# Scores of two chunks on four array quarters, level sums and low weight parts on GpSimd

## The chip, the cores and the metric

The kernel runs on one core of a Trainium2 chip. The metric is device time of one execution in microseconds: 2511.98 us, the median of three runs (2508.98 to 2515.89). One execution was recorded by the hardware profiler; it took 2509.05 us, of which 2507.3 us lie between its first and its last instruction (the span).

The engines have short names in the profile: PE is TensorE's matrix multiplication, PEld its weight loads, DVE is VectorE, ACT is ScalarE, POOL is GpSimd, and SP is SyncE, which here only issues DMAs.

## What is computed

Two transformer blocks work on one sequence of 1024 tokens of width 1024, all in fp32. The change lies in the second block, in its two gated linear attentions (four heads with 64 keys and 128 values, four heads with 64 keys and 64 values). With a cumulated log gate `b_cum` per token and key, every chunk of 64 tokens needs

```
scores = jnp.einsum('bhtd,bhsd,bhtsd->bhts', q_c, k_c, decay)   # decay = exp(b_t - b_s) for s <= t
o_c    = scores @ v_c + (q_c * exp(b_cum)) @ state
state  = exp(b_last) * state + (k_c * exp(b_last - b_cum)).T @ v_c
```

The decay depends on the pair of tokens and on the key, so the score is not one matrix product. The kernel halves the chunk six times: at level l, pairs whose tokens lie in the left and in the right half of the same piece of 64 >> l tokens are one product of k * exp(ref - b) and q * exp(b - ref), with ref the gate at the end of the left half. The diagonal is a seventh product, k with q.

Next to it the block has a projection (`w_in_2`, `w_values`), a stick-breaking attention, and an output projection (`w_out_2`).

## The kernel before

A large product in fp32 is three products in a faster format: a weight tile of 128x512 (`wr`, 256 KB) is split into a high part `wh` (ACT, L77) and a low part `wl` = wr - wh (DVE, L80), and PE multiplies hi with wl, lo with wh and hi with wh (L153, L773 to L775). `load_parts` does this for every tile, with three buffers for each of `wr`, `wh` and `wl`.

The second block is a set of Python generators, each of which yields a cost; `weave` always steps the one that is behind, and so writes one program out of four streams: `filler` (the projection's units, then the output rows), two streams `gated` (two pairs of heads each, per half of the sequence: `gla_a`, `gla_b`, `gla_c`), and `sticks`. A scheduler then orders each engine's instructions; on the chip every engine works its own list in order and waits on semaphores.

In `gla_b`, `gla_levels` makes the left and right operands of all six levels for four chunks (`XL`, 128x256 a level): two subtractions and two multiplications of 128x128 on DVE and one exponential of 128x256 on ACT for each level. Partitions 0 to 63 hold one head, 64 to 127 the other. Then, chunk by chunk, PE multiplies: levels 2 to 5 and the diagonal as 64x64 products (L1416, L1418), levels 1 and 0 as products of 16 and 32 columns (L1421), the two heads on two quarters of the array: rows 0 to 63 into PSUM partitions 0 to 63, and rows 64 to 127 into 64 to 127. Each chunk takes one of two PSUM buffers `s`, shared by both gated streams. DVE multiplies the five 64-column pieces with their masks (`mk`, 128x320, one buffer in each stream) and adds them up with a reduction (L1424) into `PT`, the stationary operand of the product with the values (L1445).

The trace records each fp32 product of this size as two MATMULs and two LDWEIGHTS: a product is two passes through its quarter.

Of the kernel before, what the change touches and what calls it, by code (L numbers as in the profile page):

```python
# [65 lines left out]
def tile_hybrid_blocks(ctx: ExitStack, tc: tile.TileContext, a: dict, out: bass.AP):  # L66
# [66 lines left out]

    def load_parts(src, shape):

        wr = wp.tile(shape, F32, tag="wr", name="wr")
        SY.dma_start(out=wr, in_=src)
        wh = wp.tile(shape, F32R, tag="wh", name="wh")
        wl = wp.tile(shape, F32R, tag="wl", name="wl")
        split(wh, wl, wr)  # L140
        return wh, wl
# [1146 lines left out]
    def gla_levels(half, jj, q, k, b, c0, c1):  # L1288
# [4 lines left out]
        q, k, b = q[:, n0:n0 + m], k[:, n0:n0 + m], b[:, n0:n0 + m]  # L1293
        for l in range(6):
# [7 lines left out]
            bl, br = v4(b)[:, :, 0, :], v4(b)[:, :, 1, :]  # L1302
            ref = bl[:, :, h - 1:h].to_broadcast([128, n, h])
            tt(v4(ar)[:, :, 0, :], ref, bl, SUB)
            tt(v4(ar)[:, :, 1, :], br, ref, SUB)
            act(ar, ar, AF.Exp, scale=1.0 / 16 if jj < 2 else 1.0)
            xl = v4(XL[:, l, :])
            tt(xl[:, :, 0, :], v4(k)[:, :, 0, :], v4(ar)[:, :, 0, :], MUL)
            tt(xl[:, :, 1, :], v4(q)[:, :, 1, :], v4(ar)[:, :, 1, :], MUL)
        return XL  # L1310

    def gla_a(half, jj):
# [13 lines left out]
        SY.dma_start(out=qk, in_=qk_d[half][jj].rearrange("a p t -> p a t"))  # L1326
        q, k = qk[:, 0, :], qk[:, 1, :]
# [54 lines left out]
    def gla_b(half, jj):  # L1382
# [18 lines left out]
        o = 0  # L1401
        for c in range(8):
            if c % 4 == 0:
                XL = gla_levels(half, jj, q, k, b, c, c + 4)
                yield YL * 4
                o = c
            cs = slice(c * 64, (c + 1) * 64)
            ps = pss_t([128, 5, 64])

            def xl(hb, l, c0, n):  # L1410
                return XL[hb:hb + 64, l, (c - o) * 64 + c0:(c - o) * 64 + c0 + n]


            for l in (2, 3, 4, 5):
                for hb in (0, 64):
                    T.matmul(out=ps[hb:hb + 64, l - 2, :], lhsT=xl(hb, l, 0, 64), rhs=xl(hb, l, 0, 64), start=True, stop=True)  # L1416
            for hb in (0, 64):
                T.matmul(out=ps[hb:hb + 64, 4, :], lhsT=k[hb:hb + 64, cs], rhs=q[hb:hb + 64, cs], start=True, stop=True)  # L1418
            for l, lc, rc, n in ((1, 0, 16, 16), (1, 32, 48, 16), (0, 0, 32, 32)):
                for hb in (0, 64):  # L1420
                    T.matmul(out=ps[hb + lc:hb + lc + n, 0, rc:rc + n], lhsT=xl(hb, l, lc, n), rhs=xl(hb, l, rc, n), start=True, stop=True)  # L1421
            mk = slot("mk", [128, 5, 64])
            tt(mk, ps, lvm, MUL)
# [308 lines left out]
```

## Time and profile before

| | |
|---|---|
| median of three runs | 2511.98 us (2508.98 to 2515.89) |
| the profiled execution | 2509.05 us, span 2507.3 us |
| busy share of the span | PE 95%, PEld 74%, DVE 67%, ACT 47%, POOL 4% |
| weave of the four streams | from about 1870 us to 2455 us of the span |
| mean granted TensorE clock | 0.981 of full speed |

An engine's busy time counts overlapping instructions once. A matmul's recorded length contains the time in which the array fills and drains, so the rate of a dense row of matmuls is read from the distance of their starts, not from their length.

### The profile page before, as it was taken

What the parts mean: (1) busy time and instruction counts of PE and PEld (TensorE: products, weight loads), DVE (VectorE), ACT (ScalarE), POOL (GpSimd) and SP (SyncE); (2) the same over time, 40 slices, a digit from 0 to 9 for tenths busy, and PEclk for the clock granted to TensorE, in tenths of its full rate; (3) what the DMA queues carried; (4) which work ended last, traced back from release to release, by engine and by line L of the source; (5) the groups of instructions that cost most, each with busy time, mean ns of one, the idle gap of its engine ahead of it and who ended that gap; (6) DMA issues with size and microseconds to landing.
All of it is one profiled execution on the core that took longest, in us unless ns stands there. A gap on an engine that the chain in (4) does not pass through costs nothing.

```text
span 2507.3 us, 40921 instructions
## 1 busy us (share of the span) xinstructions
PE 2375.0 (95%) x15310; PEld 1863.7 (74%) x15310; DVE 1688.9 (67%) x3678; ACT 1171.0 (47%) x2223; POOL 100.2 (4%) x138
## 2 busy tenths in 40 slices
PE   6989998889999999999999999999999999999997
PEld 5767776767777777778778887788877667777665
DVE  5466556667686776663885555555568988788887
ACT  4345433654433434343543333343345575656863
POOL 1001000100000000000000000000000000000000
PEclk9999999979999999999999999999999999999989
DMA  6433323555352342333463332243256335342446
GB/s 203 147 116 89 99 87 94 160 162 159 97 172 79 107 140 91 92 124 96 161 205 94 97 93 93 81 156 100 94 166 223 99 112 179 105 132 91 144 136 244
DMA packets 219997, 320.77 MB, mean 128 GB/s; under 512 B 56956, under 2 KB 95508, under 8 KB 219799
## 3 DMA queue, kind: packets, MB, share of 16 engines
q1 hardware_dynamic: 219798, 318.17, 40.5%
q8 instruction: 120, 1.97, 0.3%
q14 instruction: 79, 0.64, 0.1%
HBM read 270.88 MB, written 47.21 MB: 127 GB/s over the span
## 4 chain that ended last, share of the span: by engine, by line
PE 60%; DVE 9%; DMA 3%; issue 3%; ACT 2%; POOL 1%; SPq 0%; POOLq 0%; ACTq 0%; DVEq 0%
PE g L153 32%; PE d L153 12%; DVE wl L80 1%; PE s L1416 1%; PE R L1520 1%; PE gr L773 1%; DVE cv L83 1%; PE gr L774 1%; PE gr L775 1%; PE x L773 1%; PE x L775 1%; PE x L774 1%; DVE tmp L80 1%; PE z L1505 1%; PE po L1538 1%
## 5 line engine op out<-in xcount | busy, mean ns | idle before, releaser
L77 ACT ACTIVATE wh<-wr 128x512 fp32r<-128x512 f32 x712 | 442.8, 626 | 639.8 <-PE g L153 216.9
L153 PE MATMUL g<-hi,wl 128*128 128x512 f32 (+1 forms) x1680 | 677.1, 403 | 13.5 <-DVE lo L80 4.1
L153 PE MATMUL g<-hi,wh 128*128 128x512 f32 (+1 forms) x1680 | 667.2, 397 | 0.0
L153 PE MATMUL g<-lo,wh 128*128 128x512 f32 (+1 forms) x1680 | 665.5, 396 | 0.0
L80 DVE TENSOR_TENSOR wl<-wr,wh 128x512 fp32r<-128x512 f32 x712 | 484.7, 685 | 207.2 <-ACT wh L77 205.9
L153 PEld LDWEIGHTS g<-hi,wl 128*128 128x128 f32 (+1 forms) x1680 | 317.1, 189 | 91.0 <-issue 8.6
L153 PEld LDWEIGHTS g<-hi,wh 128*128 128x128 f32 (+1 forms) x1680 | 316.7, 188 | 71.7 <-issue 2.6
L153 PEld LDWEIGHTS g<-lo,wh 128*128 128x128 f32 (+1 forms) x1680 | 317.2, 189 | 68.5 <-issue 3.7
L83 DVE SCALAR_TENSOR_TENSOR cv<-g,CW,cv 128x511 f32<-128x511 f32 (+1 forms) x256 | 190.8, 745 | 179.3 <-ACT cv L77 179.0
L153 PE MATMUL d<-hh,wl 128*128 128x512 f32 x512 | 202.5, 399 | 12.7 <-ACT hh L77 7.5
L153 PE MATMUL d<-hl,wh 128*128 128x512 f32 x512 | 202.1, 395 | 0.1
L153 PE MATMUL d<-hh,wh 128*128 128x512 f32 x512 | 200.8, 392 | 0.0
L77 ACT ACTIVATE cv<-g,CW 128x512 f32<-128x512 f32 x128 | 99.5, 777 | 181.5 <-PE g L153 181.1
L80 DVE TENSOR_TENSOR acc<-d,acc 128x512 f32<-128x512 f32 x112 | 76.4, 689 | 94.7 <-PE d L153 94.6
L153 PEld LDWEIGHTS d<-hh,wl 128*128 128x128 f32 x512 | 95.8, 189 | 41.8 <-ACT hh L77 12.0
L153 PEld LDWEIGHTS d<-hl,wh 128*128 128x128 f32 x512 | 96.5, 188 | 23.0 <-DVE hl L80 3.6
L153 PEld LDWEIGHTS d<-hh,wh 128*128 128x128 f32 x512 | 96.6, 189 | 20.3 <-issue 0.2
L773 PE MATMUL gr<-wl,hi 128*128 128x512 f32 x200 | 83.4, 418 | 7.3 <-DVE wl L80 6.6
L774 PE MATMUL gr<-wh,lo 128*128 128x512 f32 x200 | 80.1, 400 | 0.0
L775 PE MATMUL gr<-wh,hi 128*128 128x512 f32 x200 | 79.7, 399 | 0.0
L127 POOL TENSOR_TENSOR rs<-ms,half_c 128x1 f32<-128x1 f32 x48 | 29.4, 612 | 1085.1 <-DVE ms L87 1077.2
L77 ACT ACTIVATE hh<-cv 128x512 fp32r<-128x512 f32 x64 | 40.4, 631 | 65.5 <-DVE cv L80 65.4
(508 smaller groups left out, 3475.7 us busy)
## 6 DMA issues: line engine op xcount, KB each, us to landing
wr<-in_w_up_dram SPq DMA_DIRECT2D x256, 256.0 KB, 2.7
wr<-in_w_in_dram SPq DMA_DIRECT2D x160, 256.0 KB, 2.9
wr<-in_w_down_dram SPq DMA_DIRECT2D x128, 256.0 KB, 2.6
wr<-in_w_out_dram SPq DMA_DIRECT2D x100, 256.0 KB, 3.0
wr<-in_w_values_dram SPq DMA_DIRECT2D x64, 256.0 KB, 2.9
wa<-in_w_ada_dram SPq DMA_DIRECT2D x24, 512.0 KB, 4.3
xt<-x SPq DMA_DIRECT2D x24, 512.0 KB, 4.5
xt<-in_x_dram SPq DMA_DIRECT2D x16, 512.0 KB, 3.6
```

What stands on the lines that cost most here:

```text
L77: S.activation(out=out, in_=in_, func=func, **kw)
L80: (eng or V).tensor_tensor(out=out, in0=in0, in1=in1, op=op)
L83: V.scalar_tensor_tensor(out=out, in0=in0, scalar=scalar, in1=in1, op0=op0, op1=op1)
L127: G.tensor_tensor(out=dst, in0=src, in1=half_c[0:src.shape[0], 0:src.shape[1]], op=ALU.pow)
L153: T.matmul(out=ps, lhsT=l, rhs=r, start=(first and n == 0), stop=(last and n == 3 * len(wk) - 1))
L773: T.matmul(out=p, lhsT=hi[:, k, tok], rhs=wl, start=first, stop=False)
L774: T.matmul(out=p, lhsT=lo[:, k, tok], rhs=wh, start=False, stop=False)
L775: T.matmul(out=p, lhsT=hi[:, k, tok], rhs=wh, start=False, stop=last)
L1416: T.matmul(out=ps[hb:hb + 64, l - 2, :], lhsT=xl(hb, l, 0, 64), rhs=xl(hb, l, 0, 64), start=True, stop=True)
L1505: T.matmul(out=z[:, h, :], lhsT=Ks[:, p, h, kb * 128:(kb + 1) * 128], rhs=q[:, h, off:], start=q is ql, stop=q is qh)
L1520: T.matmul(out=R[:, :, c0:c1], lhsT=m, rhs=x[:, :, c0 - off:c1 - off], start=start and x is sl, stop=x is sh, skip_group_check=not start)
L1538: T.matmul(out=po[hb:hb + 64, c0:c1], lhsT=Vh[:, kb, hd * 64:(hd + 1) * 64], rhs=ar[:, h, c0 - off:c1 - off], start=(kb == top), stop=(kb ...
```

## The change

Four things change, all in the second block.

The scores of two chunks are now multiplied together. The second chunk's heads go to the other two quarters: rows 0 to 63 into PSUM partitions 64 to 127, rows 64 to 127 into 0 to 63, in the second PSUM buffer. A pair of chunks takes both `s` buffers at once; the two heads of the second chunk lie swapped in PSUM and are swapped back when `PT` is written.

The sum over the levels is no longer a DVE reduction: POOL adds 128x128, then 128x64, and for the first chunk of a pair writes `PT` with a third addition; for the second chunk, two DVE additions of 64x64 write `PT`.

`gla_levels` makes one subtraction of 128x256 (b - ref on both halves), two exponentials of 128x128 with opposite scale, and one multiplication of 128x256 for each level. For the latter k and q lie side by side in one tile, in the order k, q, which two DMAs load instead of one.

In the weave of the four streams, `load_parts` makes the low part `wl` on POOL instead of DVE.

```diff
--- before.py
+++ after.py
@@ -131,13 +131,17 @@
         act(hi, src, AF.Copy)
         tt(lo, src, hi.bitcast(F32), SUB)
 
+
+    low_eng = [V]
+
     def load_parts(src, shape):
 
         wr = wp.tile(shape, F32, tag="wr", name="wr")
         SY.dma_start(out=wr, in_=src)
         wh = wp.tile(shape, F32R, tag="wh", name="wh")
         wl = wp.tile(shape, F32R, tag="wl", name="wl")
-        split(wh, wl, wr)
+        act(wh, wr, AF.Copy)
+        tt(wl, wr, wh.bitcast(F32), SUB, low_eng[0])
         return wh, wl
 
     def load_w(src, m=128):
@@ -1290,7 +1294,7 @@
         slot = rooms[jj < 2][0]
         n0, m = c0 * 64, (c1 - c0) * 64
         XL = slot("XL", [128, 6, m])
-        q, k, b = q[:, n0:n0 + m], k[:, n0:n0 + m], b[:, n0:n0 + m]
+        k, b = k[:, n0:n0 + m], b[:, n0:n0 + m]
         for l in range(6):
             h = 32 >> l
             n = m // (2 * h)
@@ -1299,14 +1303,14 @@
                 return t.rearrange("p (n s h) -> p n s h", s=2, h=h)
 
             ar = slot("tmp", [128, HALF], "ar")[:, 0:m]
-            bl, br = v4(b)[:, :, 0, :], v4(b)[:, :, 1, :]
-            ref = bl[:, :, h - 1:h].to_broadcast([128, n, h])
-            tt(v4(ar)[:, :, 0, :], ref, bl, SUB)
-            tt(v4(ar)[:, :, 1, :], br, ref, SUB)
-            act(ar, ar, AF.Exp, scale=1.0 / 16 if jj < 2 else 1.0)
-            xl = v4(XL[:, l, :])
-            tt(xl[:, :, 0, :], v4(k)[:, :, 0, :], v4(ar)[:, :, 0, :], MUL)
-            tt(xl[:, :, 1, :], v4(q)[:, :, 1, :], v4(ar)[:, :, 1, :], MUL)
+            ref = v4(b)[:, :, 0, h - 1:h].to_broadcast([128, n, 2 * h])
+            tt(ar.rearrange("p (n t) -> p n t", n=n), b.rearrange("p (n t) -> p n t", n=n), ref, SUB)
+            tau = 1.0 / 16 if jj < 2 else 1.0
+            for s in range(2):
+                act(v4(ar)[:, :, s, :], v4(ar)[:, :, s, :], AF.Exp, scale=tau if s else -tau)
+
+            kq = bass.AP(k.tensor, k.offset, [k.ap[0], [2 * h, n], [HALF + h, 2], [1, h]])
+            tt(v4(XL[:, l, :]), kq, v4(ar), MUL)
         return XL
 
     def gla_a(half, jj):
@@ -1323,8 +1327,9 @@
             return t.rearrange("p (c t) -> p c t", c=8)
 
         qk = slot("qk", [128, 2, HALF])
-        SY.dma_start(out=qk, in_=qk_d[half][jj].rearrange("a p t -> p a t"))
-        q, k = qk[:, 0, :], qk[:, 1, :]
+        for x in range(2):
+            SY.dma_start(out=qk[:, 1 - x, :], in_=qk_d[half][jj][x])
+        k, q = qk[:, 0, :], qk[:, 1, :]
 
         mn, e, b = tmp("mn"), tmp("e"), tmp("b")
         if is_g:
@@ -1398,31 +1403,42 @@
                                  start=True, stop=True)
                 yield YT
             stt(Sa[:, c + 1, 0:dv] if c < 7 else Sg[jj], Sa[:, c, 0:dv], ebl[:, c, :], kv[:, c % nb, :], MUL, ADD)
-        o = 0
-        for c in range(8):
+        for c in range(0, 8, 2):
             if c % 4 == 0:
                 XL = gla_levels(half, jj, q, k, b, c, c + 4)
                 yield YL * 4
-                o = c
-            cs = slice(c * 64, (c + 1) * 64)
-            ps = pss_t([128, 5, 64])
-
-            def xl(hb, l, c0, n):
-                return XL[hb:hb + 64, l, (c - o) * 64 + c0:(c - o) * 64 + c0 + n]
+
+            ps = [pss_t([128, 5, 64]) for _ in range(2)]
+            four = [(x, hb, hb ^ 64 * x) for x in range(2) for hb in (0, 64)]
+
+            def prod(l, at, lc, rc, n):
+                for x, hb, ob in four:
+                    if l < 6:
+                        o = (c % 4 + x) * 64
+                        kl, ql = XL[hb:hb + 64, l, o + lc:o + lc + n], XL[hb:hb + 64, l, o + rc:o + rc + n]
+                    else:
+                        o = (c + x) * 64
+                        kl, ql = k[hb:hb + 64, o:o + 64], q[hb:hb + 64, o:o + 64]
+                    T.matmul(out=ps[x][ob + lc:ob + lc + n, at, rc:rc + n], lhsT=kl, rhs=ql, start=True, stop=True)
 
 
             for l in (2, 3, 4, 5):
-                for hb in (0, 64):
-                    T.matmul(out=ps[hb:hb + 64, l - 2, :], lhsT=xl(hb, l, 0, 64), rhs=xl(hb, l, 0, 64), start=True, stop=True)
-            for hb in (0, 64):
-                T.matmul(out=ps[hb:hb + 64, 4, :], lhsT=k[hb:hb + 64, cs], rhs=q[hb:hb + 64, cs], start=True, stop=True)
+                prod(l, l - 2, 0, 0, 64)
+            prod(6, 4, 0, 0, 64)
             for l, lc, rc, n in ((1, 0, 16, 16), (1, 32, 48, 16), (0, 0, 32, 32)):
-                for hb in (0, 64):
-                    T.matmul(out=ps[hb + lc:hb + lc + n, 0, rc:rc + n], lhsT=xl(hb, l, lc, n), rhs=xl(hb, l, rc, n), start=True, stop=True)
-            mk = slot("mk", [128, 5, 64])
-            tt(mk, ps, lvm, MUL)
-            V.tensor_reduce(out=PT[:, c, :].unsqueeze(2), in_=mk.rearrange("p l t -> p t l"), axis=X, op=ADD)
-            yield YB
+                prod(l, 0, lc, rc, n)
+            for x in range(2):
+                mk = slot("mk", [128, 5, 64])
+                tt(mk, ps[x], lvm, MUL)
+
+                tt(mk[:, 0:2], mk[:, 0:2], mk[:, 2:4], ADD, G)
+                tt(mk[:, 0], mk[:, 0], mk[:, 1], ADD, G)
+                if x == 0:
+                    tt(PT[:, c], mk[:, 0], mk[:, 4], ADD, G)
+                else:
+                    for i0, o0 in ((0, 64), (64, 0)):
+                        tt(PT[o0:o0 + 64, c + 1], mk[i0:i0 + 64, 0], mk[i0:i0 + 64, 4], ADD)
+            yield YB * 2
         gls[half, jj] = (qt, V2, PT, Sa)
 
     def gla_c(half, jj):
@@ -1587,7 +1603,9 @@
         for half in range(2):
             yield from stick(half)
 
+    low_eng[0] = G
     weave(filler, Stream(gated(0), RG, AG), Stream(gated(2), RH, AG), Stream(sticks(), RS, AS))
+    low_eng[0] = V
     p3.close()
 
     p4 = ExitStack()
```

The lists of the engines, with what each instruction waits for. PE, between output rows and scores, before (one chunk: eight 64x64 products of the levels, two of the diagonal, six narrow ones):

```order
L773 MATMUL gr<-wl,hi 128x512
L774 MATMUL gr<-wh,lo 128x512
L775 MATMUL gr<-wh,hi 128x512
L1416 MATMUL s<-XL 64x64 x8
L1418 MATMUL s<-qk 64x64 x2
L1421 MATMUL s<-XL 16x16 x4
L1421 MATMUL s<-XL 32x32 x2
L773 MATMUL gr<-wl,hi 128x512 [waits DVE_49]
L774 MATMUL gr<-wh,lo 128x512 [waits Activation_49]
```

PE after, a pair of chunks between the projection and the stick-breaking sums (L1422 holds all score products now):

```order
L157 MATMUL g<-hi,wh 128x512
L1422 MATMUL s<-XL 64x64 [waits DVE_49]
L1422 MATMUL s<-XL 64x64
L1422 MATMUL s<-XL 64x64 [waits DVE_49,PE_49]
L1422 MATMUL s<-XL 64x64 x13
L1422 MATMUL s<-qk 64x64 x4
L1422 MATMUL s<-XL 16x16 x8
L1422 MATMUL s<-XL 32x32 x4
L1536 MATMUL R<-sl,rest_r 128x512
L1536 MATMUL R<-sh,rest_r 128x512
```

Twice the products now stand in one uninterrupted row, so PE goes over from wide to narrow products and back once for two chunks.

DVE, around the masks of two chunks, before (`mk` is the masked product, `ev` and `wl` belong to the filler):

```order
L80 TENSOR_TENSOR mk<-s,C_16659 128x320 [waits DVE_49,PE_49]
L1424 TENSOR_REDUCE PT<-mk 128x64 [waits DVE_49]
L80 TENSOR_TENSOR mk<-s,C_16659 128x320 [waits DVE_49,PE_49]
L80 TENSOR_TENSOR ev<-ev,g 128x512 [waits Activation_49]
L1424 TENSOR_REDUCE PT<-mk 128x64 [waits DVE_49]
L87 TENSOR_SCALAR tmp<-qk 128x512 [waits DMAHW3_49]
L80 TENSOR_TENSOR wl<-wr,wh 128x512 [waits DMAHW7_49,Activation_49]
```

DVE after, at one of the six pairs in which nothing stands between the masks:

```order
L83 SCALAR_TENSOR_TENSOR gt<-t,P,gt 128x256
L80 TENSOR_TENSOR mk<-s,C_16659 128x320 [waits PE_49]
L80 TENSOR_TENSOR mk<-s,C_16659 128x320 [waits DVE_49,PE_49,Pool_49]
L80 TENSOR_TENSOR PT<-mk 64x64 [waits DVE_49,Pool_49]
L80 TENSOR_TENSOR PT<-mk 64x64
L1394 COPY Sa<-Sg_16668 128x128 [waits PE_49]
L1468 TENSOR_REDUCE ssn<-tmp 128x4 [waits Activation_49]
```

The second mask and the last additions now wait for POOL, and whatever stands behind them on DVE waits with them.

POOL after, in the same place (before, its list there held only the small powers of L127):

```order
L80 TENSOR_TENSOR wl<-wr,wh 128x512 [waits DMAHW2_49,PE_49,Activation_49]
L80 TENSOR_TENSOR mk<-mk 128x128 [waits DVE_49]
L80 TENSOR_TENSOR mk<-mk 128x64 [waits Pool_49]
L80 TENSOR_TENSOR PT<-mk 128x64 [waits Pool_49]
L80 TENSOR_TENSOR mk<-mk 128x128 [waits DVE_49]
L80 TENSOR_TENSOR mk<-mk 128x64 [waits Pool_49]
L127 TENSOR_TENSOR rsn<-ssn,half_c 128x4 [waits DVE_49]
L80 TENSOR_TENSOR wl<-wr,wh 128x512 [waits DMAHW4_49,Activation_49]
```

Low parts and level sums stand in one list: a low part behind a sum waits for DVE's mask, and a sum behind a low part waits for its weights.

## Rows read from the trace of the kernel before

**Rows 1.** The page's part 4, the chain that ended last, by engine

```profile
PE 60%; DVE 9%; DMA 3%; issue 3%; ACT 2%; POOL 1%; SPq 0%; POOLq 0%; ACTq 0%; DVEq 0%
```

**Rows 2.** Busy time by stretch: stretch, length, PE, PEld, DVE, ACT, POOL (instructions), clock, DMA

```profile
1870.00:2455.00 585.00, 554.32 (x5129) 414.17 (x5128) 485.60 (x1133) 374.04 (x727) 21.32 (x20) 0.99 0.44 140
1884.00:2335.00 451.00, 436.45 (x4174) 329.78 (x4172) 375.38 (x906) 280.91 (x554) 14.48 (x14) 1.00 0.42 133
2335.00:2455.00 120.00, 105.93 (x883) 75.72 (x884) 98.77 (x201) 85.63 (x161) 6.84 (x7) 0.94 0.46 149
```

**Rows 3.** The same view, L1416's matmuls and weight loads alone

```profile
1884.00:2335.00 451.00, 44.46 (x896) 34.03 (x896) 1.00 0.42 133
```

**Rows 4.** PE's timeline around one chunk: start, length to the last end, line, count

```profile
2307.11 0.39 PE L153 MATMUL g<-lo,wh 128*128 128x512 f32 x1
2307.33 0.39 PE L153 MATMUL g<-hi,wh 128*128 128x512 f32 x1
2307.65 0.68 PE L1416 MATMUL s<-XL 64*64 64x64 f32 x16
2308.16 0.28 PE L1418 MATMUL s<-qk 64*64 64x64 f32 x4
2308.38 0.29 PE L1421 MATMUL s<-XL 64*16 64x16 f32 x12
2308.60 0.50 PE L1520 MATMUL R<-sl,rest_r 128*128 128x512 f32 x1
2308.94 0.40 PE L1520 MATMUL R<-sh,rest_r 128*128 128x512 f32 x1
```

**Rows 5.** PE's timeline in the first block, 64x64 products on other quarters

```profile
202.66 1.15 PE L576 MATMUL rb__1594<-TT,UV 64*64 64x64 f32 x32
...
205.96 0.68 PE L617 MATMUL ou<-St,AR 64*64 64x64 f32 x16
...
219.32 0.68 PE L626 MATMUL ou<-St,AR 64*64 64x64 f32 x8
```

**Rows 6.** Groups on DVE and ACT, 1870 to 2455 us: busy us, mean ns | idle before

```profile
L80 DVE TENSOR_TENSOR wl<-wr,wh 128x512 fp32r<-128x512 f32 x154 | 104.4, 686 | 27.1 <-ACT wh L77 26.9
L80 DVE TENSOR_TENSOR XL<-qk,tmp 128x128 f32<-128x128 f32 x192 | 47.4, 284 | 3.8 <-ACT tmp L77 3.2
L80 DVE TENSOR_TENSOR tmp<-tmp 128x128 f32<-128x128 f32 x192 | 45.8, 284 | 0.4 <-PE t L1366 0.2
L1424 DVE TENSOR_REDUCE PT<-mk 128x64 f32<-128x320 f32 x64 | 45.8, 719 | 0.1
...
L80 DVE TENSOR_TENSOR se<-se,C 128x256 f32<-128x256 f32 x16 | 6.7, 419 | 0.1
...
L77 ACT ACTIVATE tmp<-tmp 128x256 f32<-128x256 f32 x96 | 38.2, 412 | 31.1 <-DVE tmp L80 30.6
```

**Rows 7.** Groups on POOL, 0 to 1100 us

```profile
L127 POOL TENSOR_TENSOR rs<-ms,half_c 128x1 f32<-128x1 f32 x16 | 9.5, 596 | 133.9 <-DVE ms L87 126.0 <-DVE XT L80 7.9
L80 POOL TENSOR_TENSOR kk<-k,P 128x512 f32<-128x512 f32 x8 | 8.4, 1046 | 85.6 <-DMA k<-rkv_d 75.5 <-PE ra L495 10.1
```

**Rows 8.** Timelines of POOL and DVE where both work

```profile
134.49 1.04 POOL L80 TENSOR_TENSOR kk<-k,P 128x512 f32<-128x512 f32 x1 [10.07 <-PE ra L495]
...
135.06 0.68 DVE L80 TENSOR_TENSOR MT<-rb__1053,C 128x512 f32<-128x512 f32 x1
...
227.46 1.05 POOL L80 TENSOR_TENSOR kk<-k,P 128x512 f32<-128x512 f32 x1
...
227.54 1.52 DVE L80 TENSOR_TENSOR og<-og,rsd 128x512 f32<-128x512 f32 x1 [1.82 <-POOL rsd L127]
...
456.80 1.43 POOL L80 TENSOR_TENSOR r<-r,P 128x512 f32<-128x512 f32 x1 [7.39 <-DVE AR L80]
...
456.63 2.14 DVE L80 TENSOR_TENSOR wl<-wr,wh 128x512 fp32r<-128x512 f32 x2
```

**Rows 9.** What PE waited for, 1870 to 2455 us: total us, times, longest

```profile
PE gr L773 <- DVE wl L80: 4.2, 6, 2.2
```

## The prediction

> **What bounds the kernel now.** I read the chain that ended last first. It runs on PE for most of its length, 60% against 9% on DVE [rows 1], so time is to be had where PE has less to do, as long as nothing else is late. The change touches only the weave of the four streams; everything up to 1870 us stays. Busy time by stretch is next [rows 2]: in the 585 us of the weave PE is busy for 554 us, 95%, and DVE for 486 us, 83%. The stretch splits in two. From 1884 to 2335 us PE is busy for 436 of 451 us (97%): a pure PE limit. From 2335 to 2455 us PE falls to 88%, with DVE at 82% and ACT at 71%, and the granted clock has a dip (0.94): there the stick-breaking chain and the last heads wait on each other. Of the 1024 records of L1416, 896 lie in the first stretch [rows 3], that is 56 of the 64 chunks or 28 of the 32 pairs. The waits come last: PE lost only 4.2 us to low parts that DVE made too late [rows 9], although DVE spends 104 us on them [rows 6].
>
> **PE: what four quarters save.** One chunk stands between two wide products in [rows 4]. From its first to the next wide matmul it takes 2308.60 - 2307.65 = 0.95 us: 0.73 us for the 20 wide passes and 0.22 us for the 12 narrow ones. Around it PE loses time to the change of shape: the matmul before it lasts 0.32 us to the next start, where its neighbour takes 0.22 (+0.10), and the one behind it 0.34 (+0.12). A chunk alone thus costs 1.17 us, two 2.34, and two in a row 0.95 x 2 + 0.22 = 2.12 us.
>
> Do four quarters work at once? 16 passes on two quarters that share no rows and no columns take 0.68 us [rows 4]; 8 passes through a single quarter take the same 0.68 us (L626) [rows 5], so two run side by side. L576 sends one half of the rows into both halves of the columns, and 32 passes take 1.15 us; L617 sends both halves of the rows into one half of the columns, and 16 take 0.68 us [rows 5]. Both kinds of neighbour run at the pace of two. All four at once in 64x64 is not in the trace, but the narrow passes come at 0.22 / 12 = 18 ns each, which one or two quarters at a time would hardly give. So I take it that a pair of chunks needs 0.73 us for its 40 wide passes, 0.32 us for its 24 narrow ones (bounds 0.22, four times as parallel, and 0.44, no gain) and 0.22 us of changes: 1.27 us. The saving is 2.34 - 1.27 = 1.07 us for chunks that stood apart, 2.12 - 1.27 = 0.85 us for two in a row; I take 0.95, times 32 is 30 us. If only two quarters run at a time, the pair needs 2 x 0.73 + 0.32 + 0.22 = 2.00 us, and the saving is 0.12 to 0.34 us a pair: 4 to 11 us.
>
> A rule of the Trainium skill speaks against it: the page "TensorEngine Tiling (Array Packing)", in "Restrictions and Gotchas", says that tiles of different rows cannot write to one PSUM bank at the same time. By it the two heads of a chunk, which write to one buffer, would already take turns, and the pair would gain no more than two at a time. The trace disagrees: L1416 with one buffer and L617 with a buffer for each half both show 16 passes in 0.68 us [rows 4, 5].
>
> **DVE and ACT.** Low parts: 104 us leave DVE [rows 6]. Levels: 384 operations of 128x128, 47.4 + 45.8 = 93 us, become 192 of 128x256; a 128x256 of the same kind takes 0.419 us [rows 6], 80 us, so 13 us go. Sums: the reduction's 45.8 us go, and 64 additions of 64x64 come, between nothing and 0.284 us each; with 0.2 that is 13 us. Together DVE's 486 us become 486 - 104 - 13 - 33 = 336 us. ACT gets two 128x128 exponentials for one 128x256 of 0.412 us [rows 6]; each costs 0.21 to 0.41 us, I take 0.31, and 96 x 0.2 = 20 us more lie on an engine that is busy for 374 of 585 us [rows 2]: hidden before 2335 us, and up to 2 us (8 of 64 chunks) in the last stretch. Eight more DMAs on SP's queue load k and q apart, ahead of heads that start microseconds later; nothing.
>
> **POOL.** It gets 168 low parts (166 of 128x512). A 128x512 of that kind takes 1.046 us there [rows 7], against 0.686 us on DVE [rows 6]: 174 us. Its 160 sums are not in the trace: a 128x128 lies between a quarter of 1.046 and all of it, a 128x64 between an eighth and all; the smallest row is 0.596 us for a power of one column [rows 7]. I take 0.35 and 0.25: 46 us. So POOL works about 220 us of 565.
>
> What makes this less than a gift is [rows 8]. While POOL's 1.05 us ran, a DVE operation with two SBUF inputs started 0.08 us behind it and took 1.52 us, where 0.686 is usual [rows 6]; and a POOL operation that met DVE at work took 1.43 us, with one of the two DVE operations beside it stretched to match (2.14 us for both). The one waits for the whole of the other. So POOL's 220 us are not free beside DVE: at worst all of them hold DVE, at best none. More than half of what is left on DVE reads two SBUF tensors (levels, softplus, splits), and POOL runs 39% of the time; I take a third, 73 us.
>
> The "GPSIMD Engine Reference" of the Trainium skill ("Performance versus the Vector engine") makes GpSimd about twice as slow as VectorE in such operations; the rows here give 1.046 / 0.686 = 1.5. By the page POOL would work 166 x 1.37 + 46 = 274 us, and the lock's third would be 91 instead of 73 us.
>
> **The new waits.** There is one `mk` buffer in each stream. So the second mask waits for POOL's three sums of the first chunk, 0.85 us (bounds 0.5 and 3.1), and the last additions for two more, 0.6 us (0.4 and 2.1). In DVE's list one to two instructions stand between on average, and in six pairs none; they cover half. Left are 0.8 us a pair, 26 us of standing still in DVE (0 to 166). Behind a waiting mask stand the next levels' subtractions and the stick-breaking operations, for which PE waits. A pair also holds both score buffers, so the other stream's scores wait until the second mask is read; PE has some 20 filler matmuls between pairs, which cover that.
>
> DVE after: 336 + 73 + 26 = 435 us of some 565, 77% against 83%. It is no tighter than before, so what PE saves can come through. For the weights, POOL is 0.36 us slower per tile and meets DVE; but the queue ahead of it is shorter, and three buffers cover it. Of 104 us of low parts 4.2 us showed on PE; if POOL's 174 + 57 (a third of a microsecond of lock each) show by the same 4%, that is 9 us, 5 more than now.
>
> **Sum.** 28 pairs lie where PE is the limit: 28 x 0.95 = 27 us. The other four lie where PE has 14 us of gaps, and count nothing. 27 - 5 for later weights - 2 for ACT = 20 us. Against the profiled execution: 2509.05 - 20 = 2489 us. The median lies 2.9 us above that execution, so I forecast 2492 us. With 0.85 to 1.07 a pair and 0 to 15 us of new waits it is 2482 to 2503; this is the likeliest case's own range. Chance 50%.
>
> **Rivals.**
> 1. *The locks make DVE the limit (slower).* If POOL's 220 us hold DVE nearly in full and every wait for sums shows (1.45 x 32 = 46 us), DVE needs 336 + 220 + 46 = 602 us for a stage of 585. At its best filling, say 95%, that is 634. From 602 to 634 the kernel is 17 to 49 us slower, 2529 to 2561 us; near the lower end, since locks in which POOL gives way cost DVE nothing: 2537. It decides when more than about two thirds of POOL's time hold DVE. For it: both directions of the lock are in [rows 8], and low parts and sums share one list. Against it: an operation that reads PSUM, as the masks do, was not held, 0.68 us beside POOL's 1.04 [rows 8], and DVE has 17% of slack. Chance 25%.
> 2. *The saving does not arrive.* Two quarters at a time save 4 to 11 us; less 5 to 7 for the waits, that is between 3 us lost and 6 us won, with the middle 2510. Or all four run, and PE waits for weights and levels by as much. For it: four at once is not in a row. Against it: [rows 5]. Chance 12%.
> 3. *DVE's relief pays too.* If half of PE's 31 idle us in the weave [rows 2] go with DVE's lighter list and the full 30 us come through, it is 2512 - 30 - 15 = 2467 us. For it: [rows 9], and the last stretch, where low parts stand on the chain. Against it: the locks. Chance 13%.
>
> **Range and chances.** 0.3% is 7.5 us, about what a measurement of this kernel can tell from no change. Faster: case 1 nearly whole, rival 3 and a little of rival 2, 0.63. Within: 0.12, most of rival 2. Slower: 0.25. The range reaches from rival 3 to the lower half of rival 1, 2467 to 2532.
>
> **What would show it.** Four quarters: 32 wide passes of the levels in a row end after about 0.7 us, not 1.2. The low parts on POOL: mean near 1.05 us if DVE gives way, 1.4 and more if POOL does. The locks: 192 operations of 128x256 on DVE well above 0.42 us in the mean; 0.6 would be the third that I took, 0.8 and more rival 1. The handshake: idle time of DVE before `mk` and `PT` that ends on POOL, near 26 us. PE: busy time in the weave down by about 30 us, its idle time still 30 to 40. The forecast is wrong if PE's idle time in the weave doubles, with DVE or POOL as the releaser.

## The result and the profile after

The changed kernel takes 2572.94 us (median of 4 runs; the kernel before 2510.48 us on the same chip): 1.0248 times as long, interval 1.0223 to 1.0272. One of the four runs took 5718.59 us, for a reason that nothing here shows; the ratio leaves it out, and the other three took 2569.03 to 2573.99 us. The change makes the kernel 62 us slower, above even the 2529 to 2561 us of the rival in which POOL's locks decide. The profiled execution has a span of 2567.3 us; the weave of the four streams now ends near 2515 us instead of 2455. Lines behind `load_parts` stand 4 further down in the file than before; the score products are all L1422, the projection's L773 to L775 are L777 to L779.

The chain that ended last, by engine, of the changed kernel (answers to [rows 1]):

```profile
PE 50%; DVE 10%; issue 6%; POOL 6%; ACT 3%; DMA 3%; SPq 0%; POOLq 0%; ACTq 0%; DVEq 0%
```

PE gave up ten points of the chain, and POOL, which held 1% of it, now holds 6%. Busy time by stretch (columns as in [rows 2]), the whole weave and the two stretches of before:

```profile
1870.00:2515.00 645.00, 550.59 (x5147) 406.08 (x5145) 451.76 (x777) 383.63 (x828) 311.21 (x340) 0.96 0.40 128
1884.00:2335.00 451.00, 386.69 (x3740) 288.00 (x3739) 311.15 (x561) 253.72 (x570) 208.04 (x240) 0.95 0.37 119
2335.00:2455.00 120.00, 104.55 (x952) 74.69 (x951) 91.34 (x151) 90.66 (x177) 60.32 (x65) 0.99 0.41 135
```

From 1884 to 2335 us PE is busy for 387 us instead of 436, in the stretch that had looked like a pure PE limit, and issues 3740 matmuls there instead of 4174. The granted clock fell with it, from 1.00 to 0.95. DVE's share of the weave fell, to 452 of 645 us or 70% (77% were forecast, 83% it was), and the kernel is slower all the same. That is the line to remember.

The scores did what they should. PE's timeline around one pair (columns as in [rows 4]):

```profile
2197.12 0.39 PE L157 MATMUL g<-hi,wh 128*128 128x512 f32 x1
2197.44 0.69 PE L1422 MATMUL s<-XL 64*64 64x64 f32 x32
2197.95 0.30 PE L1422 MATMUL s<-qk 64*64 64x64 f32 x8
2198.18 0.32 PE L1422 MATMUL s<-XL 64*16 64x16 f32 x24
2198.43 0.50 PE L157 MATMUL g<-hi,wl 128*128 128x512 f32 x1
2198.76 0.40 PE L157 MATMUL g<-lo,wh 128*128 128x512 f32 x1
```

A pair takes 2198.43 - 2197.44 = 0.99 us, hardly more than a single chunk's 0.95 in [rows 4]: all four quarters run at once. The groups on ACT, DVE and POOL from 1870 to 2515 us (columns as in [rows 6]):

```profile
L80 POOL TENSOR_TENSOR wl<-wr,wh 128x512 fp32r<-128x512 f32 x158 | 221.0, 1407 | 225.8 <-ACT wh L77 221.0 <-PE R L1536 4.2
L80 DVE TENSOR_TENSOR tmp<-tmp 128x256 f32<-128x256 f32 x96 | 58.6, 627 | 2.4 <-PE t L1371 1.6
L80 DVE TENSOR_TENSOR XL<-qk,tmp 128x256 f32<-128x256 f32 x96 | 55.5, 590 | 8.1 <-ACT tmp L77 6.8 <-PE s L1422 0.9
L77 ACT ACTIVATE tmp<-tmp 128x128 f32<-128x128 f32 x192 | 48.5, 304 | 61.0 <-DVE tmp L80 60.6
L80 POOL TENSOR_TENSOR mk<-mk 128x128 f32<-128x128 f32 x64 | 37.8, 590 | 62.9 <-DVE mk L80 62.8
L80 DVE TENSOR_TENSOR PT<-mk 64x64 f32<-64x64 f32 x64 | 32.7, 511 | 16.0 <-POOL mk L80 15.2
L80 DVE TENSOR_TENSOR mk<-s,C 128x320 f32<-128x320 f32 x64 | 31.2, 487 | 53.0 <-POOL PT L80 30.2 <-PE s L1422 21.5 <-PE z L1521 1.2
L80 POOL TENSOR_TENSOR mk<-mk 128x64 f32<-128x64 f32 x64 | 22.2, 346 | 4.9
L80 POOL TENSOR_TENSOR PT<-mk 128x64 f32<-128x64 f32 x32 | 10.4, 325 | 2.4
```

A low part takes 1.41 us in the mean. That is not all contention. All low parts of this kernel (least, median and longest, in ns):

```profile
L80 POOL TENSOR_TENSOR wl<-wr,wh x168: 320/1291/2316, 1863.3 to 2530.4; 128x512 fp32r<-128x512 f32 x166, 128x64 fp32r<-128x64 f32 x2
```

The 24 low parts of 128x512 that overlap no DVE instruction at all take 1.29 us in the median too. So 1.29 us is the instruction's own length; the 1.046 us of [rows 7], which the prediction took for it, belong to a multiplication that writes plain fp32. Beside DVE it is DVE that is held most of the time: its 128x256 take 0.59 to 0.63 us in the mean (0.419 in [rows 6]), and by single records the 42 of them that start while a low part runs take 1.26 us in the median, the 132 that start while POOL stands idle 0.417. The mask reads PSUM and stays at 0.49 (0.486 before). DVE stands idle for 30 + 15 = 45 us before `mk` and `PT` because of POOL. What it looks like in one place, on POOL, DVE and PE (answers to [rows 8]):

```profile
1906.39 6.24 POOL L80 TENSOR_TENSOR wl<-wr,wh 128x512 fp32r<-128x512 f32 x3
...
1905.16 1.03 DVE L80 TENSOR_TENSOR tmp<-tmp 128x512 f32<-128x512 f32 x2
1906.30 1.28 DVE L83 SCALAR_TENSOR_TENSOR xs<-xt,rs,gbc 128x1024 f32<-128x1024 f32 x1
1907.50 1.75 DVE L80 TENSOR_TENSOR tmp<-tmp,qk 128x512 f32<-128x512 f32 x1
1909.18 2.31 DVE L80 TENSOR_TENSOR xs<-xs,shift 128x1024 f32<-128x1024 f32 x1
1911.41 0.48 DVE L80 TENSOR_TENSOR mk<-s,C 128x320 f32<-128x320 f32 x1
...
1906.33 0.32 PE L1422 MATMUL s<-XL 64*16 64x16 f32 x24
1908.76 0.50 PE L777 MATMUL gr<-wl,hi 128*128 128x512 f32 x1 [2.11 <-POOL wl L80]
```

Three low parts take 6.24 us, 2.08 each instead of 1.29. POOL and DVE take turns here: by the times shown, each instruction goes on after the other engine's has ended, and lasts for about its own time and what was left of the other's. Both are late, and PE stands for 2.11 us behind a low part. What PE and DVE waited for, 1870 to 2515 us (columns as in [rows 9]):

```profile
DVE mk L80 <- POOL PT L80: 30.2, 21, 3.0
PE gr L777 <- POOL wl L80: 21.0, 16, 3.7
DVE PT L80 <- POOL mk L80: 15.2, 26, 1.6
PE t L1476 <- DVE tmp L80: 9.8, 7, 2.2
PE z L1521 <- DVE ql L80: 9.3, 6, 3.4
```

PE is idle for 94 us of the weave (645 less 550.6), before for 31. By the releaser of each wait, DVE ended 58 us of them (before 23), POOL 22 (before none) and ACT 13 (before 7); waits of over 0.8 us number 42 instead of 13. The granted clock is at the lower of its two levels (1.2 GHz instead of 2.4) for 58 us of the weave, in twelve stretches of which each follows a wait of PE of 1.8 to 6.3 us; before it was 17 us, in three stretches.

The books of the weave, then: it is 60 us longer, because PE stands idle for 64 us more and is busy for only 4 us less. The scores' saving (some 28 us, see below) is mostly eaten inside PE's busy time by the lower clock: PE is busy for 51 us at half speed, before for 16, which is an estimated 18 us more for the same work.

### The profile page after: what moved, and what is told of

Its sections match the earlier page's. It is cut to its first block, busy times and chain, and to the rows that moved or that the text cites. A ratio compares the mean times of both kernels' runs of the same rounds, so it can differ in the third digit from the quotient of the medians.

```text
span 2567.3 us, 41184 instructions
## 1 busy us (share of the span) xinstructions
PE 2365.1 (92%) x15310; PEld 1849.7 (72%) x15310; DVE 1651.9 (64%) x3318; ACT 1179.1 (46%) x2319; POOL 401.8 (16%) x466
## 4 chain that ended last, share of the span: by engine, by line
PE 50%; DVE 10%; issue 6%; POOL 6%; ACT 3%; DMA 3%; SPq 0%; POOLq 0%; ACTq 0%; DVEq 0%
PE g L157 28%; PE d L157 12%; POOL wl L80 3%; POOL mk L80 1%; DVE tmp L80 1%; PE x L777 1%; PE x L779 1%; PE x L778 1%; DVE cv L83 1%; DVE wl L80 1%; ACT wh L77 1%; DVE mk L80 1%; ACT ev L77 1%; DVE xs L80 1%; POOL rsn L127 1%
## 5 line engine op out<-in xcount | busy, mean ns | idle before, releaser
L80 DVE TENSOR_TENSOR wl<-wr,wh 128x512 fp32r<-128x512 f32 x544 | 372.0, 686 | 170.1 <-ACT wh L77 169.0
L80 POOL TENSOR_TENSOR wl<-wr,wh 128x512 fp32r<-128x512 f32 (+1 forms) x168 | 233.4, 1398 | 236.9 <-ACT wh L77 232.1
L127 POOL TENSOR_TENSOR rs<-ms,half_c 128x1 f32<-128x1 f32 x48 | 29.1, 607 | 926.7 <-DVE ms L87 920.3
L777 PE MATMUL gr<-wl,hi 128*128 128x512 f32 x200 | 88.2, 442 | 26.9 <-POOL wl L80 22.1
L77 ACT ACTIVATE tmp<-tmp 128x128 f32<-128x128 f32 (+1 forms) x212 | 60.8, 334 | 66.4 <-DVE tmp L80 64.5
```

The lines of the kernel that those rows point to most:

```text
L77: S.activation(out=out, in_=in_, func=func, **kw)
L80: (eng or V).tensor_tensor(out=out, in0=in0, in1=in1, op=op)
L127: G.tensor_tensor(out=dst, in0=src, in1=half_c[0:src.shape[0], 0:src.shape[1]], op=ALU.pow)
L777: T.matmul(out=p, lhsT=hi[:, k, tok], rhs=wl, start=first, stop=False)
```

## The experiments

The first question is which part costs. Each part is taken back from the changed kernel, or made alone.

**Low parts back on DVE** (the rest as changed).

```diff
-    low_eng[0] = G
     weave(filler, ...)
```

> The changed kernel, but the low parts of the weights stay on DVE; four quarters, sums on POOL and one pass per level stay. Theory A (low parts on POOL are late for PE and lock DVE): most of the 62 us comes back, 2500 to 2520 us, and PE's wait for low parts falls from 21 us to some 5. Theory B (the handshake between DVE's masks and POOL's sums stops DVE): at most 20 us come back, 2550 to 2570, and DVE still waits 40 us for POOL before masks and PT. Theory C (the pairing of chunks and the new order of the lists alone are what is slow): the same as B, with few waits on POOL.

2512.23 us, 1.0015 times before (0.9999 to 1.0030). Nearly the whole loss is gone.

**Only the low parts on POOL** (the kernel before, and that one edit).

```diff
-        split(wh, wl, wr)
+        act(wh, wr, AF.Copy)
+        tt(wl, wr, wh.bitcast(F32), SUB, low_eng[0])
...
+    low_eng[0] = G
     weave(filler, ...)
```

> The kernel before with one thing changed: low parts of the weights on POOL in the weave. Theory A: 2545 to 2575 us, since neither the four quarters' saving nor the sums are there; low parts near 1.4 us each. Theory B: 2505 to 2520 us. Theory C: as B, 2505 to 2520.

2562.69 us, 1.0201 (1.0166 to 1.0236). This part alone costs about 50 us.

**Sums on DVE, low parts on POOL.**

```diff
-                tt(mk[:, 0:2], mk[:, 0:2], mk[:, 2:4], ADD, G)
...
+                    V.tensor_reduce(out=PT[:, c, :].unsqueeze(2), ...)
```

> The changed kernel, but the level sums are DVE reductions again (one for the first chunk of a pair, two of 64 partitions for the second, since its heads lie swapped); low parts stay on POOL. Theory A: still slow, 2550 to 2580 us, PE's wait for low parts stays at 20 us or more. Theory B: 2500 to 2530 us in spite of about 96 x 0.72 = 69 us of reductions. Theory C: 2560 or more.

2559.69 us, 1.0194 (1.0170 to 1.0217). The handshake of masks and sums costs little: taking the sums back gains half a per cent here (1.0248 to 1.0194). With the low parts on DVE it gains nothing that can be told from the noise: 1.0015 with the sums on POOL, 0.9994 in the next kernel, and the intervals overlap.

**Sums and low parts on DVE**: four quarters and one pass per level are left.

> Four quarters and one pass per level, but POOL gets nothing: low parts and level sums stay on DVE (three reductions of 0.72 us per pair). DVE has 23 us more of reductions than before and 13 us less of levels. Theories A and B: PE's saving of 30 us comes through for the most part, 2485 to 2505 us. Theory C: 2530 us or more.

2507.50 us, 0.9994 (0.9977 to 1.0012). So without POOL there is no loss, but no gain either; PE's saving is missing. Its weave, by stretch (columns as in [rows 2]):

```profile
1870.00:2455.00 585.00, 535.35 (x5123) 396.43 (x5124) 498.34 (x966) 377.19 (x818) 20.55 (x20) 0.97 0.44 138
```

PE is busy 19 us less than in [rows 2], and the stage is as long. From the starts of the records, without PE's waits, the time in the score products and in the changes of shape around them went from some 90 us to some 62: the 28 us are there. Against them stand 19 us more of idle time (50 instead of 31), about half of it between the score products and right behind them. The other 9 us are PE's busy time, which fell by 19 and not by 28; the granted clock is 0.97 here and 0.99 before.

The second question is how the low parts cost. The next kernels leave work out, so that their results lack a term; they serve for their times alone.

**No low parts in the weave.**

```diff
+        if low_eng[0] is G:
+            act(wh, wr, AF.Copy)
+            return wh, wh
```

> The kernel before, in the weave without low parts of weights at all: neither DVE nor POOL makes them, and PE's product with the low part reads the high part instead (so the sums lack that term; PE's work is unchanged). DVE loses 104 of its 486 us, POOL gets nothing. It is the base for the next two. If DVE's load held PE back (its 83%), the relief shows: 24 us of PE idle plus part of the last stretch go, 2480 to 2495 us. If PE alone is the limit: 2500 to 2507, only the 4 us of waits for low parts go.

2489.17 us, 0.9908 (0.9876 to 0.9940). PE multiplies by the high part a second time. 104 us less on DVE give about 24 us. Its weave, by stretch (columns as in [rows 2]), has PE at 96% and DVE at 69%:

```profile
1870.00:2455.00 585.00, 562.18 (x5194) 422.17 (x5192) 403.16 (x973) 383.61 (x743) 20.39 (x20) 0.99 0.48 149
```

**Low parts on POOL that nobody reads.**

```diff
+        tt(wl, wr, wh.bitcast(F32), SUB, low_eng[0])
+        return wh, wh if low_eng[0] is G else wl
```

> The same, but POOL makes the low parts as in the changed kernel, 166 subtractions of 128x512 into the same buffers, and nobody reads them (PE's product reads the high part). Theory lock: what costs is that POOL's instructions hold DVE's, whoever reads the result; then most of the 52 us stay, 2540 to 2562 us, DVE's 128x128 operations stay at 0.40 us in the mean (0.284 before), and PE's idle time in the weave stays above 50 us. Rival lateness: what costs is that PE gets the low part later; then it comes out as the kernel without low parts, within 10 us.

2558.69 us, 1.0181 (1.0148 to 1.0213), as slow as with readers (1.0201). So 1.0181 - 0.9908 = 2.7%, 69 us, are what POOL's instructions cost by running at all. That PE gets its low parts late adds what the intervals can't tell from nothing. Nor is it that weights come later because POOL frees their buffers later: PE waits for them (`wh`) for 2.2 us in all. PE's waits that DVE ended went from 18 us without low parts to 44. DVE's level groups in this kernel, 1870 to 2455 us (columns as in [rows 6]):

```profile
L80 DVE TENSOR_TENSOR XL<-qk,tmp 128x128 f32<-128x128 f32 x184 | 72.1, 436 | 7.0 <-ACT tmp L77 5.2
L80 DVE TENSOR_TENSOR tmp<-tmp 128x128 f32<-128x128 f32 x188 | 66.8, 401 | 2.5 <-PE t L1369 2.2
```

0.40 to 0.44 us instead of the 0.284 of [rows 6].

**POOL instructions with one SBUF input**, unread too.

```diff
+        act(wh, wr, AF.Copy)
+        if low_eng[0] is G:
+            ts(wl, wh.bitcast(F32), 1.0, MUL, eng=G)
+            return wh, wh
```

> As the one before, but POOL's 166 instructions have one SBUF input (wh times 1.0) instead of two, and again nobody reads what they write. If POOL holds DVE only with two SBUF inputs, DVE's 128x128 operations return to 0.28 to 0.30 us and the time to that of the kernel without low parts within 10 us. If any POOL instruction that reads and writes SBUF holds DVE, the time is that of the unread low parts, in proportion to POOL's busy time.

2504.77 us, 0.9967 (0.9946 to 0.9988): 15 us over no low parts, not 69, though POOL is busy for longer. Its groups on POOL and DVE, 1870 to 2455 us (columns as in [rows 6]):

```profile
L87 POOL TENSOR_SCALAR wl<-wh 128x512 fp32r<-128x512 f32 x158 | 248.3, 1581 | 258.9 <-ACT wh L77 258.8
L80 DVE TENSOR_TENSOR XL<-qk,tmp 128x128 f32<-128x128 f32 x192 | 53.5, 322 | 9.1 <-ACT tmp L77 7.5
L80 DVE TENSOR_TENSOR tmp<-tmp 128x128 f32<-128x128 f32 x192 | 52.4, 319 | 2.5 <-PE t L1372 2.0
```

By single records: a 128x128 of DVE that starts while POOL's instruction runs takes 0.283 us in the median here (194 of them), and 1.20 us beside POOL's two-input low part (71 of them, in the kernel above); apart from POOL it takes 0.284 to 0.286 us in either kernel. Against the median of the same instruction apart from POOL, all of DVE's instructions in the weave are longer by some 76 us in sum beside the two-input one and by some 19 beside the one-input one; the kernels lose 69 and 15 us. So the cost goes with what POOL's instruction does to DVE's, and that goes with the second SBUF input. That it is the input, and not the kind of instruction (TENSOR_SCALAR instead of TENSOR_TENSOR), is argued: no run parts the two. The middle result, 15 us, was in neither expectation.

The page "SBUF — State Buffer" of the Trainium skill, in "SBUF: two separate sides", says that a VectorE operation with two SBUF inputs and a GpSimd operation that reads SBUF exclude each other for a whole instruction. The low part agrees (1.20 against 0.284 us); the one-input instruction, which reads SBUF as well, does not: four in five of DVE's operations passed beside it at their usual length.

**Four quarters and one pass, without low parts.** Is DVE's load what keeps PE's saving back?

> The four quarters and the one pass per level with the sums as DVE reductions (that kernel took 2507.5 us, PE's busy time in the weave fell by 19 us and its idle time rose by as much), and without low parts of weights in the weave. Theory DVE: at 85% DVE was too late for what PE saved; with 104 us less on DVE the saving shows, 15 to 25 us under the kernel before without low parts. Rival chains: PE waits for chains through ACT, POOL and DMA that don't get shorter when DVE has less to do; then the two are within 7 us of each other.

2492.77 us, 0.9913 (0.9885 to 0.9940), the same as without low parts alone (0.9908). The theory that DVE's load keeps the saving of the paired kernel back fell here. Its weave, by stretch (columns as in [rows 2]):

```profile
1870.00:2455.00 585.00, 544.78 (x5197) 407.27 (x5195) 416.55 (x813) 389.16 (x839) 20.89 (x20) 0.98 0.48 150
```

DVE is at 71%, PE works 17 us less than in the weave without low parts, and nothing comes of it.

The third question is what single parts do.

**Four quarters alone** (three reductions for a pair instead of two).

> The kernel before with the scores of two chunks on four quarters alone; levels as before, sums as DVE reductions (three for a pair instead of two, since the second chunk's heads lie swapped: 23 us more on DVE), low parts on DVE. Theory chains: PE's time in and around the scores falls from 92 to about 62 us, and PE's waits grow by as much, because the streams' own chains through DVE and ACT set when PE's next product may start; 2502 to 2520 us. Rival PE limit: the 28 us arrive, less a few for DVE, 2485 to 2495.

2525.81 us, 1.0055 (1.0037 to 1.0074). Slower by 14 us. Its profiled execution is 17 us longer than that of before, so its weave reaches beyond the stretch shown (columns as in [rows 2]), in which PE issues 132 matmuls fewer:

```profile
1870.00:2455.00 585.00, 527.84 (x4997) 392.12 (x4996) 496.79 (x1139) 364.76 (x713) 17.63 (x18) 0.96 0.43 133
```

To the end of its weave, near 2472 us, PE is busy for 542 us, 13 less than before, and idle for 60, 30 more.

**One pass per level alone.**

> The kernel before with one subtraction, two exponentials and one product per level alone (13 us off DVE, 20 us more on ACT), scores, sums and low parts as before. From the kernel without low parts, where 104 us less on DVE gave 24 us, 13 us less should give 3, and the second exponential lies on the same chain: 2503 to 2515 us by the chains theory; the PE limit says no change, 2505 to 2512.

2509.50 us, 0.9996 (0.9981 to 1.0011): nothing to be seen. The second exponential is as free as forecast, and the 13 us off DVE pay less than can be measured. Beside the four quarters it is another matter: they alone are at 1.0055, with the one pass at 0.9994 (above), 0.6% or 15 us apart and clear of both intervals, each against the kernel before on its own chip. Where chunks are paired, the way to the level operands counts; by which wait, no run parts.

**A shorter budget for a pair** (on the kernel with sums and low parts on DVE).

```diff
-YL, YT, YB, YC = 1.2, 2.5, 2.7, 3.6
+YL, YT, YB, YC = 1.2, 2.5, 2.2, 3.6
```

> The four quarters, one pass per level, sums and low parts on DVE (2507.5 us), with the time that a pair of chunks claims in the weave's clock lowered from 5.4 to 4.4 units, since PE now needs 1.1 us less for it. The filler's share between pairs shrinks and the gated heads come earlier. If the fixed order of PE's list was what gave the saving back (made for longer scores), it shows here: 2485 to 2500. If the chains' latencies give it back, less filler between the steps of a chain makes PE wait more: 2505 to 2525.

2513.10 us, 1.0003 (0.9991 to 1.0014). The gated heads' last scores come at 2406 us instead of 2439, and the end does not move: stick-breaking and the filler end where they did.

**The mask in two halves instead of the reduction.**

```diff
+                    for i0, o0 in ((0, 64), (64, 0)):
+                        tt(mk[o0:o0 + 64], ps[x][i0:i0 + 64], lvm[i0:i0 + 64], MUL)
```

> The same kernel with the old budget; the second chunk's heads are swapped back by the mask's product (two of 64 partitions) instead of by two reductions, so DVE has one reduction of 0.72 us less and one mask of 0.49 us more a pair, 7 us less in all and 0.23 us less from the scores to the values. Theory chains: two per cent of DVE's load, 1 to 4 us faster than 2507.5, 2502 to 2508. If DVE's load has nothing to do with it: 2507.

2513.55 us, 1.0004 (0.9992 to 1.0015). Inconclusive: 7 us less on DVE are too few to see.

The fourth question: does the saving fail to come, or does the pairing eat it?

**Pairs on two quarters** (order, buffers and reductions of the four quarters alone).

```diff
-            four = [(x, hb, hb ^ 64 * x) for x in range(2) for hb in (0, 64)]
+            four = [(x, hb, hb) for x in range(2) for hb in (0, 64)]
```

> As the four quarters alone (which took 1.0055 of before), but both chunks of a pair on the same two quarters; the order, the two PSUM buffers held at once and the three reductions of a pair stay. It parts what the pairing and its 23 us more on DVE cost from what the quarters save. Theory pairing: the saving of 28 us does arrive and the pairing costs more; then this one is 20 to 28 us slower than the four quarters, 2540 to 2555. Theory chains: PE's time does not matter here, both wait for the same chains; 2522 to 2532.

2526.03 us, 1.0058 (1.0037 to 1.0078), against 1.0055 with four quarters. By the starts, the time in and around the scores is 15 to 18 us longer here than there, and the kernel takes as long. Where chunks are paired, this much of PE's time in the scores does not count.

**Fewer products, nothing paired.**

```diff
-            for l in (2, 3, 4, 5):
+            for l in (2,):
...
-            tt(mk, ps, lvm, MUL)
+            tt(mk, ps[:, 0:1].to_broadcast([128, 5, 64]), lvm, MUL)
```

> The kernel before with the products of levels 3, 4 and 5 left out (12 of a chunk's 20 wide passes, about 0.44 us of PE each, 28 us in 64 chunks), and the mask reading the first piece five times in their place, so that DVE, ACT and the order of the list are unchanged: the PE saving of the change without its pairing. Theory pairing (PE is the limit before): 2483 to 2492 us. Theory chains (PE is not the limit before): within 10 us of before, 2500 to 2511.

2501.93 us, 0.9956 (0.9942 to 0.9969): 11 us, near the bound of the second theory. The scores' time fell by some 30 us; about a third of it arrives. (The scores no longer wait for levels 3 to 5 either, but before PE waited for level operands for 1.4 us in all.) Part of the rest is clock: the mean granted clock of these executions is 0.976 in the median, of those before 0.981. Half a per cent of 2500 us is 12 us, an upper estimate, since PE stands idle for part of that time.

**Fewer products and no low parts.**

> The same without low parts of weights in the weave (PE reads the high part twice; 104 us less on DVE; alone that gave 0.9908 of before, 24 us). Theory pairing: both add, 2455 to 2468 us. Theory chains: 2480 to 2490, as without low parts alone. If DVE's load is what kept PE's saving from coming, the two together give more than the sum of each alone.

2464.42 us, 0.9809 (0.9789 to 0.9828). Against no low parts alone (0.9908) that is 1.0%, 25 us: with DVE lighter, most of PE's saving arrives, and the two together (47 us) give more than each alone (24 + 11). The granted clock is back as well, at 0.983. The same stretch as above (columns as in [rows 2]), of which the weave ends near 2410 us here:

```profile
1870.00:2455.00 585.00, 550.61 (x4495) 411.61 (x4493) 421.80 (x1003) 387.28 (x756) 21.95 (x23) 0.98 0.50 157
```

**Both budgets shorter.**

```diff
-TB, MB, RH, YS1, YS2 = 3, 1, 1.5, 1.2, 1.7
+TB, MB, RH, YS1, YS2 = 3, 1, 1.5, 1.1, 1.55
```

> The kernel with four quarters, one pass per level, sums and low parts on DVE and the shorter budget for a pair (1.0003 of before; its gated heads ended 30 us earlier, but stick-breaking and the end of the weave did not), with the stick-breaking stream's budgets lowered by 8% too, so that all three streams come earlier against the filler. If the order is what gives the saving back: 2485 to 2503. If the chains' latencies do: 2507 to 2520.

2518.27 us, 1.0019 (1.0003 to 1.0035). It is not the order's budgets either, as far as these two numbers go. No version that does all of the work is measurably faster than the kernel before.

## Why the prediction was wrong

The step that failed is the one behind DVE's sum: "It is no tighter than before, so what PE saves can come through." With it the sum charged 5 us for PE's new waits, all of them for weights, and nothing for the chains that run through DVE; 64 us came. And the 27 us of saving, counted in full, did not arrive. The prediction had named the sign itself, PE's idle time doubled with DVE or POOL as the releaser: it tripled, and DVE and POOL ended 80 of its 94 us. Points 1 and 3 are the two failures; the others say how the remaining terms came out.

1. *Busy share is not lateness.* DVE's share fell below that of before, and a third of POOL's time as hold was a fair size: 73 us were taken, some 88 came, and the mark of 0.6 us for a 128x256 was met with 0.59 to 0.63. But a hold adds to the moment at which an instruction of a chain ends, and PE waits for that moment. I had charged the locks to DVE's list, where there was room, and nothing to the chains that run through it. With no reader of POOL's results, 69 us are lost against no low parts at all, and 104 us taken off DVE give back 24: the net 45 to 50 us are the loss of the low parts alone.

2. *POOL's own times and the wait for weights were mis-sized.* A low part takes 1.29 us without any DVE instruction beside it, not 1.046; it is 1.9 times DVE's 0.686, not 1.5. Additions of 128x128 and 128x64 take 0.46 and 0.32 us when DVE is idle, 0.35 and 0.25 were taken. POOL's 220 us became 291. So the mark "1.4 and more if POOL does" give way, which the mean of 1.41 seems to meet, misleads: three in four low parts ran at their own length, and it was mostly DVE that waited. "5 more than now": PE's waits for low parts went from 4.2 to 21.0 us, 17 more. Taken alone that wait adds nothing that can be measured, as the unread low parts show (1.0181 against 1.0201).

3. *PE's saving is right in size and did not arrive.* 0.95 us a pair were forecast; the pair of 0.99 us beside a chunk of 0.95 gives 2 x 0.95 - 0.99 = 0.91 us and one change of shape (0.22), and 28 us are missing from the scores in the kernel without POOL. But 97% busy in the first stretch was read as "a pure PE limit", so that each microsecond off PE would be one off the kernel. Of a saving of some 30 us without pairing 11 arrived; with DVE relieved, 25. PE at 97% was the fullest engine, not the only limit: DVE's chains held the kernel too, and the clock took some of the rest. With pairing nothing arrives, on two quarters or four, and with DVE at 71% too. So pairing, with the third reduction that it brings, costs what the quarters save. Which of its features does it stays open: two PSUM buffers held at once, one `mk` buffer for two masks in a row, two chunks' filler lumped behind them, or the reduction. Nor is it parted from the clock: four quarters alone ran at 0.975 and pairs on two quarters at 0.976, against 0.981 before, which is up to an estimated 15 us, as much as they are slower. PE's waits between the scores and right behind them are 8 to 9 us longer than before in the two kernels with four quarters and with sums and low parts on DVE, but only 1 to 3 us on two quarters, so they are not the whole of it.

4. *Handshake:* 26 us of DVE's idle time forecast, 45 measured; with the low parts out of POOL's list it is 31 (18.6 before `mk` and 12.4 before `PT`). Beside the low parts it costs half a per cent of the kernel, without them nothing that can be measured.

5. *Levels and ACT:* as forecast. The two exponentials take 0.304 us each (0.31 taken), and the one pass per level moves nothing by itself, though 15 us beside the four quarters.

6. *The clock* was in no term. The weave from 1884 to 2335 us had a granted clock of 1.00 before and has 0.95 now, and over the weave PE's work at half speed is an estimated 18 us longer, on top of the waits. PE's idle time was counted once, and its price was more.

The rival of the locks came nearest: its mechanism is shown. Its reasoning, that DVE would be full, is not: DVE had 30% to spare. Why the whole is above even that rival's 2529 to 2561 us, no run divides up; the lower clock is one part that it lacked.

## What to carry to other kernels

Before work moves to POOL beside a busy DVE, count the SBUF inputs on both sides: two against two took turns for whole instructions here (1.20 us where 0.284 is usual), and the delay was paid on the chains although both engines had time left. Take an instruction's price from a row of the same operation and types, read where the other engine is idle. An engine that is busy for 97% is not proof that a saving on it arrives; leave its work out (without the new structure) and see what the kernel gives back, see it again with the next engine relieved, and read the granted clock beside each time. And when two units are merged to fill an array, first run the merge without the filling, since the merge had a price of its own here (1.0058 without the filling).

## What the runs showed of the hardware that was not expected

- A one-input POOL instruction (1.49 us without DVE beside it) leaves DVE nearly alone: two-input 128x128 operations that start during it take 0.283 us in the median, beside a two-input one of POOL 1.20 us. Four in five stay at their usual length and the longest took 0.73 us, so some are held for a part of it.
- The same shape on POOL has two prices: a multiplication of 128x512 that writes fp32 takes 1.046 us, the subtraction that writes the fp32r low part 1.29, both without DVE's hold.
- A pair of chunks on four quarters, 64 passes in two PSUM buffers, takes 0.99 us, one chunk of 32 passes on two quarters 0.95.
- Additions on POOL cost 0.590 us for 128x128 and 0.325 to 0.346 for 128x64 in the mean of the changed kernel; where no DVE instruction overlaps them, 0.46 and 0.32.
- The granted clock fell where PE waited more, though not in proportion: from 1884 to 2335 us it is 1.00 before (PE idle for 15 us), 0.98 with the low parts alone on POOL (45), 0.96 with pairs on two quarters (31), 0.95 with the whole change (64).
